# Six PSUM banks in one ring, token loads sent together, and new paces for the filler of a two-scan block

## The chip, the cores and the metric

One NeuronCore of one Trainium2 chip runs the kernel. The metric is the device time of one execution in microseconds. TensorE (PE), VectorE (DVE), ScalarE (ACT), GpSimd (POOL) and SyncE (SP, which here only issues DMA transfers) each take their own instructions in the order in which they stand in the program; they meet through semaphores.

## The reference

A layer of a backbone: 2048 tokens and a prefix of 256 context tokens, 1024 channels. After an adaptive norm one projection `w_in` gives the inputs of three mixers and of a gate; the mixers' outputs, times the gate, go through `w_out`.

```
p = (layer_norm(x) * (1 + scale) + shift) @ w_in      # also for ctx
pv, u, fh, g = split(p)
y = rwkv7_scan(shift3(u), 2 directions)               # state (64 x 64) per head, 6 heads
    S = S*w - (S kk) (kk*a)^T + v k^T ;  y = S r
o = hgrn2_scan(fh, 2 directions)                      # chunks of a gated linear attention, 6 heads
    S = exp(g_last)*S + (k exp(g_last - g))^T i
mix = concat(pool(pv), readout(y), rms(o)) * silu(g)
out = layer_norm(ALPHA*x + gate * (mix @ w_out))
```

## The kernel before

Products in float32 are made of three products of split operands (high by high, low by high, high by low): a block of 128 channels by up to 512 tokens is 24 matmuls over eight k tiles. There are four stages. The first (to 511 us) projects what the first scan needs and computes its chunk factors. The second (511 to 1395) is the rwkv scan: 2304 tokens in 36 chunks of 64, both directions in the same step. The third (to 1926) is the hgrn scan in ten windows, n = 0 to 9. The fourth reads out, norms, gates and multiplies by `w_out`.

**The filler.** The rest of the projection, 22 blocks of weights by three parts of 768 tokens, runs on PE beside both scans (`filler`, matmuls at L567, PSUM tile `fps` in a ring of two of its own). It hands over six matmuls at a time. At the beginning of a part it splits the part's tokens: for each of the eight k tiles a load into `fxs` (two buffers, L529), a ScalarE cast into `fxh` (L213) and a DVE subtraction into `fxl` (L214). The load for k + 2 is issued once k is split; the last two load the next part's first ones. Weights come as `fwf` (512 KB, one buffer, L217), cast by ScalarE, subtracted by POOL into `fwl`. Sinks of two kinds transpose on PE (L597 and L626) through a bank of the scan.

**The scan.** An iteration n runs step n, and prepares later chunks: `start` makes the scores of a chunk seven steps ahead (matmuls at L720, two banks `pa` a direction, each emptied by a masked copy of DVE at L722 into `at`); `gather` writes blocks of them out and `solve` inverts them for four chunks together on DVE (L777 multiplies, L780 adds, some 62 instructions a group), spread over two iterations in portions of seven between PE's work; `merge` (L829, L839) completes the inverse on PE for the next step; `late` transposes keys (L742). Seven iterations, n = -7 to -1, stand before step 0. `step` begins with the `py` matmuls (L856, L862), then `pu` (L872), the state `zp` (L881) and the output `y2` (L897). PSUM has eight banks: `psa` (scores, merge, transposes), `psy`, `psu` and the filler's ring have two each. An allocation in a ring waits until the tile that many allocations before it is read.

**Order.** PE's order is written by hand (`manual_schedule`): the loop over n calls the generators in turn, and `pace` runs the filler by a share of `R_FIL[1]` at four points of an iteration (0.22, 0.34, 0.22, 0.22), so many portions of six matmuls. `R_FIL[0]` portions run before the loop. The other engines' orders are set by a scheduler.

**The hgrn scan.** A window has fourteen slots; each slot runs parts of `hlevels` (scores `pl`, L1043) and `hsteps` (transposes `kt`, outputs `po` at L1102 and L1105, state products `ps` at L1115, added to `sbd` by DVE at L1120), then the filler by `H_FIL`. `po` is filled over two steps, copied by ScalarE into `os` (L1109) and sent by POOL's queue (L1110). In window 8 the rest of the filler runs at slot 0, then `out_weights`: for each of eight blocks a load of `w_out` into `fwf` (L1131), times the gate on POOL (L1132), a split by ScalarE and DVE into the tiles of the filler's tokens (768 columns) and into own ones (256). The readout loads with `ya`, `yb`, `oa`, `ob` (L1214), the gate `gt` (L1227) and the pooled part `mx` (L1233), which DVE multiplies (L1234).

## Time and profile before

| | us |
|---|---|
| median of three runs | 2161.99 (2156.2 to 2167.65) |
| profiled execution | 2169.2 |
| its span, first to last instruction | 2167.3 |
| PE busy | 1866.9 (86%) |
| DVE busy | 1439.7 (66%) |
| ScalarE busy | 930.9 (43%) |
| POOL busy | 797.8 (37%) |

The profiled execution is 0.33% above the median. Its span leaves out 1.9 us around the first and the last instruction. The mean granted clock of PE is 0.909 of full speed. Busy shares are means over stages with different limits: the questions are, for each stage, which engine is busiest and what PE waited for last. A wait is written under the instruction that waited, with the one that released it; the idle time in brackets in a timeline is that of the engine before the row.

### The profile page before, as it was taken

What the parts mean: (1) busy time and instruction counts of PE and PEld (TensorE: products, weight loads), DVE (VectorE), ACT (ScalarE), POOL (GpSimd) and SP (SyncE); (2) the same over time, 40 slices, a digit from 0 to 9 for tenths busy, and PEclk for the clock granted to TensorE, in tenths of its full rate; (3) what the DMA queues carried; (4) which work ended last, traced back from release to release, by engine and by line L of the source; (5) the groups of instructions that cost most, each with busy time, mean ns of one, the idle gap of its engine ahead of it and who ended that gap; (6) DMA issues with size and microseconds to landing.
All of it is one profiled execution on the core that took longest, in us unless ns stands there. A gap on an engine that the chain in (4) does not pass through costs nothing.

```text
span 2167.3 us, 46917 instructions
## 1 busy us (share of the span) xinstructions
PE 1866.9 (86%) x18498; PEld 1581.6 (73%) x18498; DVE 1439.7 (66%) x3037; ACT 930.9 (43%) x1763; POOL 797.8 (37%) x729
## 2 busy tenths in 40 slices
PE   3788899994979988989889897989999998869996
PEld 1677788892857767878768775877787877758886
DVE  2678898885266475675484763167976777669762
ACT  3876786653213333333323233445455555223331
POOL 0144355545211332232232331454443445324653
PEclk7899999996989998999989897999998995589998
DMA  6544444327545567556545544443232333346531
GB/s 245 183 143 146 141 129 126 106 74 237 163 132 149 165 173 202 154 167 177 151 133 167 141 117 139 142 131 90 78 105 80 98 108 109 124 141 199 184 127 59
DMA packets 285156, 305.32 MB, mean 141 GB/s; under 512 B 84932, under 2 KB 243780, under 8 KB 283912
## 3 DMA queue, kind: packets, MB, share of 16 engines
q1 hardware_dynamic: 274920, 271.90, 42.1%
q10 hardware_dynamic: 4896, 17.83, 2.4%
q0 software_dynamic: 5120, 12.59, 1.9%
q8 instruction: 146, 2.39, 0.5%
q14 instruction: 74, 0.61, 0.1%
HBM read 205.49 MB, written 96.74 MB: 139 GB/s over the span
## 4 chain that ended last, share of the span: by engine, by line
PE 33%; DVE 23%; DMA 9%; issue 4%; ACT 3%; POOL 3%; SPq 1%; POOLq 0%; DVEq 0%; ACTq 0%
PE fps L567 14%; DVE o L780 5%; DVE tm L777 4%; PE po L1278 2%; PE pl L1043 2%; DVE sbd L1120 2%; PE po L1105 1%; DMA m<-sd 1%; DVE tot L1075 1%; PE po L1102 1%; DVE at L722 1%; PE py L856 1%; DMA nn<-so 1%; PE pa L720 1%; DVE ml L1222 1%
## 5 line engine op out<-in xcount | busy, mean ns | idle before, releaser
L214 POOL TENSOR_TENSOR fwl<-fwf,fwh 128x1024 fp32r<-128x1024 f32 x66 | 160.1, 2426 | 398.1 <-ACT fwh L213 299.0
L567 PE MATMUL fps<-fxh,fwh 128*128 128x256 f32 (+1 forms) x952 | 228.6, 374 | 29.8 <-ACT fxh L213 22.1
L567 PE MATMUL fps<-fxl,fwh 128*128 128x256 f32 (+1 forms) x952 | 222.1, 365 | 0.0
L567 PE MATMUL fps<-fxh,fwl 128*128 128x256 f32 (+1 forms) x952 | 214.5, 360 | 0.4 <-POOL fwl L214 0.4
L567 PEld LDWEIGHTS fps<-fxh,fwh 128*128 128x128 f32 x952 | 159.1, 200 | 60.5 <-ACT fxh L213 25.5
L567 PEld LDWEIGHTS fps<-fxl,fwh 128*128 128x128 f32 x952 | 160.8, 199 | 27.2 <-issue 4.6
L567 PEld LDWEIGHTS fps<-fxh,fwl 128*128 128x128 f32 x952 | 159.4, 198 | 25.9 <-issue 0.7
L1120 DVE SCALAR_TENSOR_TENSOR sbd<-sbd,tot,ps 64x64 f32<-64x64 f32 x432 | 120.4, 279 | 54.4 <-PE ps L1115 44.1
L1038 ACT COPY qb<-qp 64x384 f32<-64x384 f32 x192 | 99.8, 520 | 120.9 <-PE pl L1043 90.2
L902 POOL TENSOR_TENSOR ys<-ys,pp 64x384 f32<-64x384 f32 x64 | 74.1, 1158 | 199.5 <-ACT ys L899 187.7
L330 PE MATMUL ps<-xh,wh 128*128 128x258 f32 x768 | 125.6, 304 | 18.1 <-ACT wh L213 12.4
L780 DVE TENSOR_TENSOR o<-o,tm 96x31 f32<-96x31 f32 (+15 forms) x279 | 130.6, 468 | 8.1
L777 DVE TENSOR_TENSOR tm<-m,o 96x31 f32<-96x31 f32 (+15 forms) x279 | 109.6, 393 | 36.6 <-DMA m<-sd 29.0
L330 PEld LDWEIGHTS ps<-xh,wh 128*128 128x128 f32 x768 | 106.1, 198 | 31.3 <-ACT wh L213 13.8
L722 DVE TENSOR_TENSOR at<-pa,cst 128x384 f32<-128x384 f32 x144 | 74.1, 548 | 78.3 <-PE pa L720 78.0
L330 PE MATMUL ps<-xh,wl 128*128 128x258 f32 x768 | 118.9, 294 | 0.0
L1072 POOL TENSOR_TENSOR ks<-ks,tot 128x384 f32<-128x384 f32 x90 | 86.3, 964 | 86.5 <-PE pl L1043 78.9
L330 PE MATMUL ps<-xl,wh 128*128 128x258 f32 x768 | 116.2, 290 | 0.0
L1043 PE MATMUL pl<-qb,ks 128*64 128x64 f32 x2304 | 102.4, 248 | 13.4 <-POOL ks L1072 9.9
L821 DVE STREAM_TRANSPOSE nn<-nn 32x192 f32<-32x192 f32 x36 | 13.2, 367 | 146.6 <-DMA nn<-so 138.1
L330 PEld LDWEIGHTS ps<-xh,wl 128*128 128x128 f32 x768 | 104.9, 196 | 5.7 <-issue 5.2
L1043 PEld LDWEIGHTS pl<-qb,ks 128*64 128x64 f32 x2304 | 88.6, 158 | 24.7 <-POOL ks L1072 10.5
(230 smaller groups left out, 4441.9 us busy)
## 6 DMA issues: line engine op xcount, KB each, us to landing
fwf<-in_w_in_dram SPq DMA_DIRECT2D x66, 512.0 KB, 4.1
xt<-in_x_dram ACTq DMA_DIRECT2D x32, 512.0 KB, 5.0
s_kr<-kr SPq DMA_DIRECT2D x54, 256.0 KB, 2.4
s_bk<-bk SPq DMA_DIRECT2D x54, 256.0 KB, 2.5
bks<-s_bk SPq DMA_DIRECT2D x72, 192.0 KB, 2.8
krs<-s_kr SPq DMA_DIRECT2D x72, 192.0 KB, 3.0
bk<-s_bk SPq DMA_DIRECT2D x72, 192.0 KB, 2.7
kr<-s_kr SPq DMA_DIRECT2D x72, 192.0 KB, 3.2
```

The costliest lines, as they stand in the source:

```text
L214: eng.tensor_tensor(out=wl, in0=wf, in1=wh.bitcast(F32), op=ALU.subtract)
L330: PE.matmul(ps[:, 0:TG + 2], a[:, k, :], b[:, k, :], start=(i == 0), stop=(i == 23))
L567: PE.matmul(ps[:, 0:n], a[:, k, :], b[k][:, o:o + n], start=(i == 0), stop=(i == 23))
L722: V.tensor_tensor(out=at[:, h], in0=pa[h], in1=cst[:, C_MASK[d]].unsqueeze(1).broadcast_to([P, NPR, P]), op=ALU.mult)
L777: V.tensor_tensor(out=tv, in0=m[:, j:j + 1, j + 1:32].broadcast_to([nrow, na, nb]), in1=o[:, 0:na, j:j + 1].broadcast_to([nrow, na, nb]), ...
L780: V.tensor_tensor(out=o[:, 0:na, j + 1:32], in0=o[:, 0:na, j + 1:32], in1=tv, op=ALU.subtract)
L902: G.tensor_tensor(out=ys[vr], in0=ys[vr], in1=pp[d][vr], op=ALU.add)
L1038: S.copy(out=qb[hh, :, :, h, :].rearrange("q p c (i b) -> q (p c) i b", b=b), in_=src[hh].rearrange("q p (c i j b) -> q (p c) i j b", c=nc ...
L1043: PE.matmul(pl[64 * (c % 2):64 * (c % 2) + 64, :, p, c // 2, :], ks[:, p, CH * c:CH * c + CH], qb[:, p, c, :, :], start=True, stop=True)
L1072: eng.tensor_tensor(out=v_, in0=v_, in1=tv[:, :, :, 1 - par:2 - par].broadcast_to([P, NPR, nb, b]), op=ALU.mult)
L1120: V.scalar_tensor_tensor(out=sn[hh, p, hh], in0=so_[hh, p, hh], scalar=tot[hh, p, c:c + 1], in1=ps[hh, p, :], op0=ALU.mult, op1=ALU.add)
L1278: PE.matmul(po, mix[k][a][:, tj], wo[k, 0][b][:, 0:512], start=(i == 0), stop=(i == 23))
```

## The change

Four things change.

One: in the rwkv scan `psa`, `psy` and `psu` become one ring of six banks, from which scores, merges, transposes, `py`, `pu`, `zp` and `y2` are taken in the order of the program. In the hgrn scan `psl`, `psk`, `pso` and `pss` become one ring of six. The filler's own two banks stay.

Two: in the filler the first two k tiles of a part are loaded into `fxs` as before; the six others are loaded into the tiles `fxl` themselves, all at once, and split in place; the next part's first two are loaded after the second split.

Three: the paces. `R_FIL` is 10 before step 0 and 7.1 from it, for 7.6; `H_FIL` is 2.0, 1.8 and 0.85 for 2.2, 1.9 and 1.0. In PE's order this makes 540 filler matmuls before step 0 for 438 (221,184 columns for 175,104), of them 312 before the scores of the fourth chunk for 264 (129,024 columns for 110,592) and 198 from there to the first merge for 150 (76,800 for 56,832). Between the first and the last step they are 1440 for 1548 (580,608 columns for 628,224). In a window of the hgrn scan from the fourth on they are 72 for 84, and the last one stands at the beginning of window 8 for that of window 7. The first L720 stands behind 120 of them in both.

Four: `out_weights` is two generators. Columns 768 to 1024, into own tiles, run in windows 4 and 5, the others behind the filler's end, with loads of 384 KB for 512. The gate row has a tile of its own and is loaded at the stage's beginning. `os` has one buffer for two.

```
-R_FIL = (20, 7.6)
-H_FIL = (2.2, 1.9, 1.0)
+R_FIL = (20, 10, 7.1)
+H_FIL = (2.0, 1.8, 0.85)
...
-        xs = [load(parts[0], k) for k in range(2)]
+        def ahead(part):
+            return [load(part, k, fp.tile([P, FTOK], F32, name="fxs", bufs=2)) for k in range(2)]
+        xs = ahead(parts[0])
...
+            xh = [big.tile([P, FTOK], F32R, name=f"fxh{k}") for k in range(KB)]
+            xl = [big.tile([P, FTOK], F32R, name=f"fxl{k}") for k in range(KB)]
+            src = xs + [load(part, k, xl[k].bitcast(F32)) for k in range(2, KB)]
             for k in range(KB):
-                xh.append(big.tile([P, FTOK], F32R, name=f"fxh{k}"))
-                xl.append(big.tile([P, FTOK], F32R, name=f"fxl{k}"))
-                split(xs[k % 2][:, 0:n_all], xh[k][:, 0:n_all], xl[k][:, 0:n_all], V)
-                if k + 2 < KB:
-                    xs[k % 2] = load(part, k + 2)
-                elif pi + 1 < len(parts):
-                    xs[k % 2] = load(parts[pi + 1], k % 2)
+                split(src[k][:, 0:n_all], xh[k][:, 0:n_all], xl[k][:, 0:n_all], V)
+                if k == 1 and pi + 1 < len(parts):
+                    xs = ahead(parts[pi + 1])
...
-        psa = ph.enter_context(tc.tile_pool(name="psa", bufs=2, space=PSUM, reuse_waits="tile"))
-        psy = ph.enter_context(tc.tile_pool(name="psy", bufs=2, space=PSUM, reuse_waits="tile"))
-        psu = ph.enter_context(tc.tile_pool(name="psu", bufs=2, space=PSUM, reuse_waits="tile"))
+        psa = ph.enter_context(tc.tile_pool(name="psa", bufs=6, space=PSUM, reuse_waits="tile"))
+        def bank(shape, **k):
+            return psa.tile([P, 512], F32, name="pa")[:, 0:NPR * P].rearrange(shape, **k)
...
-                py.append(psy.tile([P, NPR, 2, CH], F32, name="py"))
+                py.append(bank("q (p h e) -> q p h e", p=NPR, h=2))
...
-            pace(k * R_FIL[1])
+            pace(k * R_FIL[1 if n < 0 else 2])
...
-        psl = ph.enter_context(tc.tile_pool(name="psl", bufs=2, space=PSUM, reuse_waits="tile"))
-        pst = ph.enter_context(tc.tile_pool(name="psk", bufs=1, space=PSUM, reuse_waits="tile"))
+        pst = ph.enter_context(tc.tile_pool(name="psk", bufs=6, space=PSUM, reuse_waits="tile"))
-        pso = ph.enter_context(tc.tile_pool(name="pso", bufs=1, space=PSUM, reuse_waits="tile"))
-        pss = ph.enter_context(tc.tile_pool(name="pss", bufs=2, space=PSUM, reuse_waits="tile"))
...
-                        os_ = stp.tile([P, 384], F32, name="os")
+                        os_ = stp.tile([P, 384], F32, name="os", bufs=1)
...
-        def out_weights():
-            gtb = fp.tile([P, KB, P], F32R, name="fwh", bufs=2).bitcast(F32).rearrange("q k c -> q (k c)")
-            SP.dma_start(out=gtb, in_=s_gate.partition_broadcast(P))
+        gtb = bigl.tile([P, D], F32, name="gtb")
+        SP.dma_start(out=gtb, in_=s_gate.partition_broadcast(P))
+        def out_weights(j):
+            pool, nm_, c = ((big, "fx", slice(0, FTOK)), (bigl, "wo", slice(FTOK, D)))[j]
+            n = c.stop - c.start
             for k in range(KB):
...
+                wf = fp.tile([P, KB, P], F32, name="fwf").rearrange("q k c -> q (k c)")[:, 0:n]
+                SP.dma_start(out=wf, in_=w_out[P * k:P * k + P, c])
+                G.tensor_tensor(out=wf, in0=wf, in1=gtb[:, c], op=ALU.mult)
...
+                    if n in (4, 5) and si % 3 == 1:
+                        run(ow1, 1)
...
+            run(ow1)
             run(ow)
```

How this stands in the engines' rows is shown at three places. First SP where the filler begins, at about 502 us of the trace. `fwf<-in_w_in_dram` is the filler's first load of weights, `fxs` and `fxl` are loads of tokens, `bks` and `krs` are operands of the first scores, `s_kr`, `s_bk` and `s_bon` are written by the first stage. Before:

```order
L217 DMA fwf<-in_w_in_dram 128x1024
L432 DMA s_bon<-t 128x256
L415 DMA s_kr<-kr 128x4x128
L529 DMA fxs<-s_x 128x256
L529 DMA fxs<-s_x 128x512
L416 DMA s_bk<-bk 128x4x128
L415 DMA s_kr<-kr 128x4x128
L529 DMA fxs<-s_x 128x256
L529 DMA fxs<-s_x 128x512
L416 DMA s_bk<-bk 128x4x128 x2
L432 DMA s_bon<-t 128x256
L529 DMA fxs<-s_x 128x256
```

After:

```order
L528 DMA fxl_6036<-s_x 128x512
L528 DMA fxl_6037<-s_x 128x256
L528 DMA fxl_6037<-s_x 128x512
L528 DMA fxs<-s_x 128x256
L528 DMA fxs<-s_x 128x512
L528 DMA fxs<-s_x 128x256
L528 DMA fxs<-s_x 128x512
L711 DMA bks_6005<-s_bk 128x384
L712 DMA krs_6004<-s_kr 128x384
L711 DMA bks_6010<-s_bk 128x384
L712 DMA krs_6009<-s_kr 128x384
L217 DMA fwf<-in_w_in_dram 128x1024
```

The first load of weights stood ahead of the loads of six token tiles; it now stands behind all of them, behind the next part's first two k tiles and behind four loads of the scan.

Second SP at the border ahead of the filler's last part. `bk`, `kr` and `uv` are loads of the scan, `so` is written by a solve and `s_g` by the filler. Before:

```order
L529 DMA fxs<-s_x 128x512
L529 DMA fxs<-s_x 128x256
L529 DMA fxs<-s_x 128x512
L586 DMA s_g<-fe 128x512
L529 DMA fxs<-s_x 128x256
L733 DMA bk_15339<-s_bk 128x384
L733 DMA bk_15343<-s_bk 128x384
L783 DMA so<-o 96x1024
L529 DMA fxs<-s_x 128x512
L529 DMA fxs<-s_x 128x256
L734 DMA kr_15555<-s_kr 128x384
L217 DMA fwf<-in_w_in_dram 128x1024
```

After:

```order
L588 DMA s_g<-fe 128x512
L528 DMA fxl_15225<-s_x 128x512
L528 DMA fxl_15225<-s_x 128x256
L528 DMA fxl_15226<-s_x 128x512
L528 DMA fxl_15226<-s_x 128x256
L528 DMA fxl_15227<-s_x 128x512
L528 DMA fxl_15227<-s_x 128x256
L528 DMA fxl_15228<-s_x 128x512
L528 DMA fxl_15228<-s_x 128x256
L737 DMA bk_15319<-s_bk 128x384
L737 DMA bk_15323<-s_bk 128x384
L814 DMA uv_15389<-s_vt 64x384
```

The token loads stood one by one among the scan's transfers, each behind the split that freed its buffer; now the twelve loads of six k tiles stand in a row (four of them ahead of the piece shown), and the loads of the scan behind them.

Third DVE at the end of the hgrn scan. `fxl<-fwf,fxh` is the last split of the output weights, `sbd` the state updates, `mx<-mx,gt` the product of pooled part and gate for the readout. Before, where window 8 is still running:

```order
L1045 COPY_PREDICATED sc_21085<-cst,pl 128x384
L1072 TENSOR_TENSOR qp_21080<-qp_21080,tot_21352 128x96x4
L1120 SCALAR_TENSOR_TENSOR sbd_16282<-sbd_16281,tot_21104,ps 64x64 x6
L1234 TENSOR_TENSOR mx<-mx,gt 128x512 x2
L1045 COPY_PREDICATED sc_21079<-cst,pl 128x192x2
L1072 TENSOR_TENSOR qp_21074<-qp_21074,tot_21406 128x48x8
L1120 SCALAR_TENSOR_TENSOR sbd_16281<-sbd_16282,tot_21104,ps 64x64 x6
```

After, at the last updates of window 9:

```order
L214 TENSOR_TENSOR fxl_21515<-fwf,fxh_21514 128x768
L1124 SCALAR_TENSOR_TENSOR sbd_16241<-sbd_16240,tot_21669,pa 64x64 x6
L1124 SCALAR_TENSOR_TENSOR sbd_16240<-sbd_16241,tot_21669,pa 64x64 x6
L1124 SCALAR_TENSOR_TENSOR sbd_16243<-sbd_16242,tot_21689,pa 64x64 x6
L1124 SCALAR_TENSOR_TENSOR sbd_16242<-sbd_16243,tot_21689,pa 64x64 x6
L1124 SCALAR_TENSOR_TENSOR sbd_16241<-sbd_16240,tot_21669,pa 64x64 x6
L1242 TENSOR_TENSOR mx<-mx,gt 128x512
L1124 SCALAR_TENSOR_TENSOR sbd_16240<-sbd_16241,tot_21669,pa 64x64 x6
L1242 TENSOR_TENSOR mx<-mx,gt 128x512
L1124 SCALAR_TENSOR_TENSOR sbd_16243<-sbd_16242,tot_21689,pa 64x64 x6
L1124 SCALAR_TENSOR_TENSOR sbd_16242<-sbd_16243,tot_21689,pa 64x64 x6
```

The two products of `mx` stood ahead of most of window 8's work; they now stand between the last updates of the state, behind the last split of the output weights.

## Rows read from the trace of the kernel before

**Rows 1.** Busy us (instructions) of each engine in three stretches, PE clock, DMA share.

```profile
core 0: us, PE busy (x) PEld busy (x) DVE busy (x) ACT busy (x) POOL busy (x), PEclk, DMA share, GB/s
...
511.00:559.00 48.00, 31.04 (x124) 23.84 (x126) 7.55 (x20) 10.29 (x14) 13.09 (x14) 0.73 0.62 194
...
652.00:1395.00 743.00, 651.46 (x7949) 545.61 (x7948) 443.37 (x993) 246.70 (x521) 206.64 (x183) 0.94 0.55 155
1395.00:1926.00 531.00, 484.52 (x5707) 401.84 (x5706) 374.88 (x867) 250.53 (x445) 229.96 (x194) 0.87 0.32 100
```

**Rows 2.** Waits of PE in the scan: us in total, times, longest.

```profile
PE pa L829 <- DVE at L722: 31.4, 12, 5.4
PE pa L829 <- DVE nn L821: 11.7, 1, 11.7
PE pa L720 <- DVE at L722: 10.0, 11, 2.4
PE pa L626 <- DVE at L722: 9.4, 3, 4.3
PE pa L597 <- DVE at L722: 7.8, 3, 4.2
```

**Rows 3.** Timeline of PE: start, us, instruction; in brackets idle time before it.

```profile
652.07 1.50 PE L856 MATMUL py<-zbd,kr 128*128 128x128 f32 x12
...
965.94 0.57 PE L829 MATMUL pa<-nn,at 32*32 32x32 f32 x24 [3.44 <-DVE at L722]
...
1388.67 1.50 PE L856 MATMUL py<-zbd,kr 128*128 128x128 f32 x12
```

**Rows 4.** Timeline of DVE inside one step with an inversion.

```profile
956.60 0.55 DVE L722 TENSOR_TENSOR at<-pa,cst 128x384 f32<-128x384 f32 x1
957.07 1.04 DVE L780 TENSOR_TENSOR o<-o,tm 96x231 f32<-96x231 f32 x1
958.03 0.54 DVE L722 TENSOR_TENSOR at<-pa,cst 128x384 f32<-128x384 f32 x1
...
965.35 1.01 DVE L722 TENSOR_TENSOR at<-pa,cst 128x384 f32<-128x384 f32 x2
```

**Rows 5.** Groups of the page: the inversion of the solves.

```profile
L780 DVE TENSOR_TENSOR o<-o,tm 96x31 f32<-96x31 f32 (+15 forms) x279 | 130.6, 468 | 8.1
L777 DVE TENSOR_TENSOR tm<-m,o 96x31 f32<-96x31 f32 (+15 forms) x279 | 109.6, 393 | 36.6 <-DMA m<-sd 29.0
```

**Rows 6.** Timeline of PE at the beginning of the filler.

```profile
544.29 1.98 PE L567 MATMUL fps<-fxh,fwh 128*128 128x512 f32 x8
546.11 1.98 PE L567 MATMUL fps<-fxh,fwl 128*128 128x512 f32 x8
...
558.84 0.94 PE L720 MATMUL pa<-krs,bks 64*128 64x128 f32 x12
```

**Rows 7.** Timeline of PE at the borders between the filler's parts.

```profile
802.18 1.64 PE L567 MATMUL fps<-fxl,fwh 128*128 128x512 f32 x6
...
828.33 2.08 PE L567 MATMUL fps<-fxh,fwh 128*128 128x256 f32 x8
...
1293.76 1.98 PE L567 MATMUL fps<-fxl,fwh 128*128 128x512 f32 x8
...
1328.64 3.62 PE L567 MATMUL fps<-fxh,fwl 128*128 128x512 f32 x8
```

**Rows 8.** The same columns as the first group, in window 7.

```profile
1780.00:1840.00 60.00, 53.61 (x562) 44.71 (x560) 43.05 (x98) 28.37 (x53) 28.55 (x21) 0.52 0.36 108
```

**Rows 9.** Timeline of POOL: first and last multiplication of the output weights.

```profile
1744.86 2.37 POOL L1132 TENSOR_TENSOR fwf<-fwf,fwh 128x1024 f32<-128x1024 f32 x1 [5.24 <-DMA s_g<-fe]
...
1836.60 2.35 POOL L1132 TENSOR_TENSOR fwf<-fwf,fwh 128x1024 f32<-128x1024 f32 x1 [2.67 <-DVE tot L1075]
```

**Rows 10.** The tile os: duration in ns; its transfers to landing.

```profile
L1109 ACT COPY os<-po x32: 462/479/481, 1523.4 to 1924.9; 128x384 f32<-128x384 f32 x32
...
DMA to landing us min/median/max: 2.1/3.2/5.4
```

More of the change, by code (lines that the diff above doesn't have):

```diff
@@ L523, in filler, with load @@
     def filler(parts, blocks):
-        def load(part, k):
-            xs = fp.tile([P, FTOK], F32, name="fxs", bufs=2)
+        def load(part, k, xs):
             o = 0
@@ L867, in step @@
             yield 1
-            pu = psu.tile([P, NPR, 2, CH], F32, name="pu")
+            pu = bank("q (p h e) -> q p h e", p=NPR, h=2)
             for p, h in heads_:
@@ L877, in step @@
             if n + 1 < NCH:
-                zp = psu.tile([P, 2, NPR, CH], F32, name="pu")
+                zp = bank("q (d p e) -> q d p e", d=2, p=NPR)
                 for d in range(2):
@@ L891, in step @@
             if lat:
-                y2 = psu.tile([P, NPR, 2, CH], F32, name="pu")
+                y2 = bank("q (p h e) -> q p h e", p=NPR, h=2)
                 for p, h in heads_:
@@ L1039, in scores @@
                            in_=src[hh].rearrange("q p (c i j b) -> q (p c) i j b", c=nch, j=2, b=b)[:, :, :, par, :])
-                pl = psl.tile([P, 2, NPR, nm, CH // 2], F32, name="pl")
+                pl = bank(384, "q (h p m t) -> q h p m t", h=2, p=NPR, m=nm)
                 for p in range(NPR):
@@ L1050, in hlevels @@
             if lat:
-                pd = [psl.tile([P, NPR, nm, CH], F32, name="pl") for _ in range(2)]
+                pd = [bank(384, "q (p m t) -> q p m t", p=NPR, m=nm) for _ in range(2)]
                 for h in range(2):
@@ L1098, in hsteps @@
                     if s % 2 == 0:
-                        po = pso.tile([P, NPR, 2, CH], F32, name="po")
+                        po = bank(384, "q (p h e) -> q p h e", p=NPR, h=2)
                     for p in range(NPR):
@@ L1107, in hsteps @@
                     if s % 2 == 1:
-                        os_ = stp.tile([P, 384], F32, name="os")
+                        os_ = stp.tile([P, 384], F32, name="os", bufs=1)
                         S.copy(out=os_, in_=po.rearrange("q p h e -> q (p h e)"))
                         QO.dma_start(out=s_o[d, t0 + P * m:t0 + P * m + P, :], in_=os_)
-                ps = pss.tile([P, NPR, CH], F32, name="ps")
+                ps = bank(192, "q (p e) -> q p e", p=NPR)
                 for p in range(NPR):
```

18 lines of the change are left out of this document (7 added, 11 removed).

## The prediction, made before the changed kernel was run

> **What bounds the kernel now.** I read the table of stages first: in which stage is the matmul engine (PE) idle, and which other engine is as long? Over the scan of 36 steps, 652 to 1395 us, PE is busy 651.46 of 743 us, VectorE (DVE) 443.37, the others far less [rows 1]. So PE is the longest engine and stands idle for 91.5 us; in the second scan (1395 to 1926) it is idle for 46.5. In the stretch in which the filler begins, 511 to 559, it is idle for 17 us. Next the waits of PE: which ended last? In the scan the largest is L829, the first matmul of a merge, for the L722 copies of DVE: 31.4 us in 12 waits. The filler's own transposes at L626 and L597 wait for the same copies, 9.4 and 7.8, and the score matmuls at L720 10.0: together 58.6 us [rows 2]. L829 does not read what L722 writes; it asks for a PSUM bank that L722 has to empty, and the ring "psa" has two banks, so that each request waits for the one but one ahead of it. Then the timelines: L829 at 965.94 stood 3.44 us [rows 3], while DVE issued the copies of one chunk at 956.60, 958.03 and 965.35, each between pieces of the inversion (tm, o) [rows 4]. So PE waits for a copy that lies on a busy DVE behind work that nobody waits for at that moment.
>
> The length of a step: the first step begins at 652.07 and the last at 1388.67 [rows 3], 736.6/35 = 21.05 us. DVE's floor in a step with an inversion: L777 and L780 take 130.6 + 109.6 = 240.2 us [rows 5] for nine groups, 26.7 a group, spread over two steps, 13.3 each. What else DVE does in the scan is 443.4 less eight groups, 230 us or 6.4 a step. So 19.7 us for a step that inverts (16 of them), and no step of that kind can be much under 20. The others are bounded by PE.
>
> **The change part by part.** The price of a filler product of 512 columns: eight start at 544.29 and the next eight at 546.11 [rows 6], 1.82/8 = 0.2275 us.
>
> *Start, to the first score matmuls at 558.84* [rows 6]: 0. Products stand there for tokens now, and the tokens' loads go out at once after the change; but by the order they, the next part's four loads and four of the scan stand ahead of the first weight load on SP, which stood far ahead before. Earlier tokens meet later weights, and the same 120 matmuls lie ahead of the first L720. The 17 idle us bound it [rows 1]; half of them either way, -8 to +8, is an estimate.
>
> *Products before step 0*: 438 become 540, by columns +46,080, or 46,080/512 x 0.2275 = 20.5 us. The solve of the first group begins with the fourth chunk; 18,432 more columns lie ahead of that, +8.2, and nothing hides them. From there to the first merge 19,968 more lie beside the solve, whose end PE awaited for 11.7 us [rows 2]: 8.9 us of products fit into that and cost nothing. Of the last 7,680 (3.4 us) I take 1.5 as seen. Lead-in +9.7; bounds +8 (all covered) and +20 (nothing covered).
>
> *The scan*: (a) 47,616 columns fewer between the first step and the last, 93 x 0.2275 = -21. (b) The ring of six banks: thirteen requests an iteration, so that a request waits for the sixth ahead of it. L829 and the filler's transposes then wait for the first direction's copies, not the second's, some 9 us sooner on DVE (956.60 against 965.35 [rows 4]). The 31.4, 9.4 and 7.8 are 48.6 us; the 10.0 of L720 stay, as its sixth is the copy just before. I take two thirds, -32: the rest comes back where DVE at its 19.7 us is behind anyway, as then the next request, the py of the next step, waits for the second direction's copies. (c) The borders between parts. Between the last product of part 0 at 802.18 and the first of part 1 at 828.33 lie 26 us, and between 1293.76 and 1328.64, where products run in a row again, 35 [rows 7]. Six of eight token loads now go out together instead of each after the split of the one two ahead of it. I take 20 us less in sum; but 12 issues in a row stand in SP's queue ahead of the scan's own loads (kr, uv, gathers), for which I give back 5: -15, bounds +5 and -30. (d) Clock: PE was granted 0.94 of full speed over the scan [rows 1], that is about 89 us of half clock, and half clock stands where PE had stood idle. With 50 us less idle: -5, bounds 0 and -20. Together -73. Bounds: -35 (waits move to the py, borders gain nothing) and -105 (nearly all idle time goes).
>
> *The second scan*: the paces fall, by 0.2 a slot in the first window, 0.1 in two and 0.15 from the fourth. By the order that last is 84 to 72 products a window; so some 80 products leave windows 0 to 6, and with the 12 that are left over from the first scan some 90 go into windows 7 and 8. -5 for the first three and -10 for the next four (48 products at 0.2 each). In window 7 before, 1780 to 1840, PE had no products and was granted 0.52 of its clock, [rows 8], against 0.87 over the whole of this stage [rows 1]. It took about 58 us at half clock; at full clock its own work is near 30 and 72 products add 16: -10. Window 8 gets some 20 products: +4. PE's waits for copies there fall with the shared ring: -6. (e) Three quarters of the output weights go through POOL, ScalarE and DVE only after the last product, so in window 8 and later: eight blocks, which before took from 1744.86 to 1836.60 [rows 9]; at 7.5 us each (less POOL work, 768 columns for 1024) 60 us from the beginning of window 8, ending some 10 us before the second scan's end instead of 80. The readout's tiles lie over theirs, and by the order DVE multiplies mx between the last updates of the state: +4, bounds 0 and +12. Together -23; bounds -8 and -45.
>
> **The sum**: 0 + 9.7 - 73 - 23 = -86.3, against the profiled execution: 2169.2 - 86.3 = 2082.9. The median of the runs, 2161.99, is 0.9967 of the profiled 2169.2, so 2076. Of the bounds, taken as independent, about 45 us remain to either side.
>
> **Rivals.** *DVE keeps PE waiting anyway.* The copies stay in DVE's row behind the inversion's pieces; if the second direction's copies are as late as before, py of the next step waits instead of L829. For it: in [rows 4] the copy of 956.60 is followed by an o of 1.04 us and the next copy starts only after it, in their order. Against it: py stands 6 to 7 us behind L829 with products between. Then the -32 and half of the borders' gain (7) are lost: -47, 2122 profiled, 2115. Beside this: the Trainium skill, "PSUM — Partial Sum Buffer", section "Engine vs sequencer instructions", says that the queues of ScalarE, VectorE and GpSimdE are strictly first in, first out. By that rule a larger ring cannot move a copy ahead of the inversion; the trace agrees (956.60, 957.07, 958.03 stand one behind the other), and it is why a third of (b) stays in my sum.
>
> *Work only moves.* PE is busy 88% in the scan, the number of products is the same, and what leaves the steps comes back in the lead-in: +20 there, -21 in the scan, the waits reappear under other names, and 10 us remain from the second scan. About 2158. Against it: the idle time is there to be filled.
>
> *Slower: the shared ring in the second scan.* A po bank is held over two steps and emptied by the ScalarE copy into os, which has one buffer now instead of two; so a copy must wait until the transfer of the copy before it has landed, 3.2 us in the median [rows 10], and the six-bank ring hands this to whatever PE asks for next. 32 copies x (3.2 + 0.5) = 118 us: 2082.9 + 118 = 2201, 2194 as a median. It decides from 86/32 = 2.7 us a copy. Against it: a copy would have to follow the one before within some 4 us to wait at all, and 32 copies between 1523.4 and 1924.9 [rows 10] lie 12.5 us apart in the mean.
>
> *Better*: nearly all of the scan's idle time goes and the clock holds: -140, 2022.
>
> **Chances.** Forecast 0.60, DVE 0.22, only moves 0.07, slower 0.05, better 0.06. The range from 2030 to 2130 takes in the forecast with its bounds and the DVE rival, and leaves out about 0.18. A measurement of this kernel can tell about 0.5% from no change: faster by more 0.88, within it 0.07, slower 0.05.
>
> **What would show it.** In the waits of PE: L829 behind L722 near nothing, py behind L722 under 20 us in sum. If py has 30 or more, the DVE rival holds. The first step near 662, and steps of 19 us in the mean up to the last. Borders of 15 to 20 us. PE at full clock through window 7. The first L720 within 8 us of 558.8. The last multiplication of the output weights some 10 us before the last po; if it is later and DVE's mx stands idle before the last sbd, (e) was too small. ScalarE's os copies waiting for their own transfers would speak for the slower rival. Wrong altogether it would be if the step stayed at 21 us with fewer products in it: then PE was not the bound.

## The result and the profile after

The changed kernel takes 2085.82 us in the median of four runs (2084.24 to 2086.05) against 2164.82 (2156.2 to 2168.75): a ratio of 0.9639, with an interval from 0.9607 to 0.9671. That is about 78 us less; the forecast was 2076. The profiled execution took 2086.04 us with a span of 2084.0. Where the time went, by the marks of the two traces:

| | before | after | difference | forecast |
|---|---|---|---|---|
| first score matmuls | 558.84 | 555.24 | -3.6 | 0 |
| step 0 | 652.07 | 658.95 | +6.9 | +9.7 |
| step 0 to step 35 | 736.6 | 672.9 | -63.7 | -73 |
| step 35 to the last state product | 536.2 | 504.0 | -32.2 | -27 |
| from there to the end | 242.4 | 248.2 | +5.8 | +4 |

The forecast's -23 for the second scan's stage is split here into its -27 and the +4 of the readout. Single profiles scatter in these rows. Five profiles of kernels with the changed code up to step 0 have the first scores at 554.3 to 557.3 and step 0 at 658.8 to 661.5; a second profile with the old code up to there has 556.4 and 650.6. So the -3.6 is about what single profiles differ by, and the +6.9 may be 9. The busy us of each engine (PE, weight loads, DVE, ScalarE, POOL, each with its instructions), the granted clock of PE, the DMA share and GB/s in three stretches of the changed kernel, to be held against [rows 1]:

```profile
511.00:555.00 44.00, 28.02 (x120) 21.68 (x120) 4.40 (x15) 9.31 (x12) 11.91 (x5) 0.83 0.58 187
...
659.00:1332.00 673.00, 613.70 (x7743) 518.45 (x7742) 439.49 (x988) 235.29 (x504) 199.74 (x182) 0.94 0.59 167
1332.00:1836.00 504.00, 477.04 (x5798) 395.02 (x5797) 370.18 (x864) 250.21 (x445) 231.78 (x200) 0.90 0.35 107
```

In the first scan PE is idle for 59 us instead of 91, and busy for 38 us less in these stretches (32 from step 0 to step 35); in the second its idle time fell from 46 to 27. What PE waited for in the first scan (us in total, times, longest), which answers to [rows 2]:

```profile
PE pa L724 <- DVE at L726: 17.5, 5, 5.1
PE pa L628 <- DVE fe L625: 13.5, 2, 7.4
PE pa L876 <- ACT pp L870: 11.9, 9, 3.9
PE pa L833 <- DVE nn L825: 9.8, 2, 6.2
```

L833 (L829 before) no longer waits for the copies (L726, before L722) at all. The scores at L724 wait for them longer than before, 17.5 against 10.0. The timeline of PE shows the beginning, the first merge, the two borders, and the first and last step, as [rows 3, 6, 7] do for before:

```profile
522.12 3.68 PE L569 MATMUL fps<-fxh,fwh 128*128 128x512 f32 x8 [13.85 <-ACT fwh L213]
...
525.64 2.02 PE L569 MATMUL fps<-fxh,fwl 128*128 128x512 f32 x8
...
555.24 0.94 PE L724 MATMUL pa<-krs,bks 64*128 64x128 f32 x12
...
646.75 0.28 PE L833 MATMUL pa<-nn,at 32*32 32x32 f32 x2 [6.17 <-DVE nn L825]
...
658.95 1.50 PE L860 MATMUL pa<-zbd,kr 128*128 128x128 f32 x12
...
757.57 1.66 PE L569 MATMUL fps<-fxl,fwh 128*128 128x512 f32 x6
...
776.28 2.04 PE L569 MATMUL fps<-fxh,fwh 128*128 128x256 f32 x8
...
1248.41 2.00 PE L569 MATMUL fps<-fxl,fwh 128*128 128x512 f32 x8
...
1271.86 2.65 PE L569 MATMUL fps<-fxh,fwh 128*128 128x512 f32 x8
...
1331.82 1.39 PE L860 MATMUL pa<-zbd,kr 128*128 128x128 f32 x11
```

PE stands 13.85 us for the first block of weights, which the tokens now precede, and the first scores come 3.6 us earlier all the same. The wait for the first solve is 6.17 instead of 11.7. From the start of the last product of a part to the start of the first of the next it is 17.5 and 21.8 us, against 24.9 and 23.7 before (the second was followed by single products until 1328.64).

### The profile page after: what moved, and what is told of

It reads as the page before. It is cut to its first block, busy times and chain, and to the rows that moved or that the text cites. A ratio compares the mean times of both kernels' runs of the same rounds, so it can differ in the third digit from the quotient of the medians.

```text
span 2084.0 us, 47024 instructions
## 1 busy us (share of the span) xinstructions
PE 1841.7 (88%) x18498; PEld 1563.7 (75%) x18498; DVE 1433.6 (69%) x3037; ACT 927.0 (44%) x1762; POOL 799.7 (38%) x737
## 4 chain that ended last, share of the span: by engine, by line
PE 40%; DVE 17%; DMA 7%; issue 5%; POOL 3%; ACT 3%; SPq 1%; POOLq 0%; ACTq 0%; DVEq 0%
PE fps L569 17%; DVE tm L781 2%; DVE o L784 2%; PE po L1286 2%; PE pa L1047 2%; PE pa L724 2%; PE pa L860 2%; DVE sbd L1124 2%; PE pa L876 1%; PE pa L1109 1%; PE pa L866 1%; PE pa L1106 1%; DVE tot L1079 1%; DMA fwf<-in_w_out_dram 1%; DMA fwf<-in_w_in_dram 1%
## 5 line engine op out<-in xcount | busy, mean ns | idle before, releaser
L569 PEld LDWEIGHTS fps<-fxh,fwh 128*128 128x128 f32 x952 | 157.1, 198 | 54.5 <-ACT fwh L213 18.8
L781 DVE TENSOR_TENSOR tm<-m,o 96x31 f32<-96x31 f32 (+15 forms) x279 | 123.3, 442 | 38.3 <-DMA m<-sd 30.5
L1124 DVE SCALAR_TENSOR_TENSOR sbd<-sbd,tot,pa 64x64 f32<-64x64 f32 x432 | 120.5, 279 | 38.4 <-PE pa L1119 28.3
L726 DVE TENSOR_TENSOR at<-pa,cst 128x384 f32<-128x384 f32 x144 | 74.2, 548 | 75.1 <-PE pa L724 74.7
L784 DVE TENSOR_TENSOR o<-o,tm 96x31 f32<-96x31 f32 (+15 forms) x279 | 114.6, 411 | 8.0
L1076 POOL TENSOR_TENSOR ks<-ks,tot 128x384 f32<-128x384 f32 x90 | 86.6, 967 | 76.5 <-PE pa L1047 66.4
L330 PEld LDWEIGHTS ps<-xl,wh 128*128 128x128 f32 x768 | 102.8, 193 | 4.9 <-issue 4.6
L1047 PE MATMUL pa<-qb,ks 128*64 128x64 f32 x2304 | 94.5, 236 | 9.0 <-POOL ks L1076 6.4
L404 POOL TENSOR_TENSOR kr<-t 128x256 f32<-128x256 f32 x54 | 47.4, 878 | 134.0 <-ACT t L391 74.9
```

What stands on the lines that cost most here:

```text
L330: PE.matmul(ps[:, 0:TG + 2], a[:, k, :], b[:, k, :], start=(i == 0), stop=(i == 23))
L404: G.tensor_tensor(out=kr[:, :, pr], in0=c4(kk), in1=e_k, op=ALU.mult)
L569: PE.matmul(ps[:, 0:n], a[:, k, :], b[k][:, o:o + n], start=(i == 0), stop=(i == 23))
L726: V.tensor_tensor(out=at[:, h], in0=pa[h], in1=cst[:, C_MASK[d]].unsqueeze(1).broadcast_to([P, NPR, P]), op=ALU.mult)
L781: V.tensor_tensor(out=tv, in0=m[:, j:j + 1, j + 1:32].broadcast_to([nrow, na, nb]), in1=o[:, 0:na, j:j + 1].broadcast_to([nrow, na, nb]), ...
L784: V.tensor_tensor(out=o[:, 0:na, j + 1:32], in0=o[:, 0:na, j + 1:32], in1=tv, op=ALU.subtract)
```

## The experiments

Twelve kernels, one of them the changed kernel once more, were run in three groups, each beside the kernel before on the same chip. The first group takes one part out of the changed kernel, the second puts one part alone into the kernel before, the third asks about the end, the start and the second scan's paces. Their stages, in us of one profiled execution each:

| kernel | step 0 at | first scan | second scan | behind it | ratio to before (interval) |
|---|---|---|---|---|---|
| before | 652.1 | 736.6 | 536.2 | 242.4 | 1 |
| changed | 659.0 | 672.9 | 504.0 | 248.2 | 0.9639 (0.9607 to 0.9671) |
| changed, old rings | 661.2 | 690.1 | 505.5 | 244.1 | 0.9721 (0.9669 to 0.9773) |
| changed, old pace of the scan | 649.1 | 694.1 | 518.5 | 241.2 | 0.9694 (0.9646 to 0.9741) |
| changed, old token loads | 661.2 | 678.7 | 507.9 | 243.3 | 0.9658 (0.9607 to 0.9708) |
| changed, old second scan | 661.5 | 673.1 | 540.7 | 241.0 | 0.9733 (0.9679 to 0.9788) |
| before, new ring alone | 649.1 | 705.2 | 540.3 | 239.7 | 0.9884 (0.9856 to 0.9912) |
| before, new pace alone | 663.1 | 696.8 | 520.5 | 240.6 | 0.9824 (0.9785 to 0.9862) |
| before, new loads alone | 649.1 | 721.9 | 530.0 | 239.2 | 0.9920 (0.9892 to 0.9948) |
| before, new second scan alone | 650.6 | 731.1 | 519.3 | 244.0 | 0.9900 (0.9873 to 0.9926) |
| changed, again | 661.2 | 674.2 | 502.5 | 241.4 | 0.9626 (0.9595 to 0.9658) |
| changed, os in the fwh tiles | 661.5 | 673.2 | 502.2 | 263.1 | 0.9720 (0.9691 to 0.9749) |
| the same, first weights ahead | 657.6 | 670.1 | 501.6 | 259.4 | 0.9686 (0.9652 to 0.9720) |
| changed, old paces of the second scan | 658.8 | 670.8 | 493.0 | 240.5 | 0.9590 (0.9552 to 0.9629) |

One unit of 0.001 is 2.2 us. The second scan's stage is from step 35 to the last state product. How far a single profile can be trusted, the rows with equal code show: the old first scan took 736.6 and, with only the second scan changed, 731.1 us; the changed one 670.8 to 674.2 in five profiles with the same code up to there; the old second scan 520.5 to 540.7 in five.

### One part taken out

**The scan's rings.**

```
-        psa = ph.enter_context(tc.tile_pool(name="psa", bufs=6, space=PSUM, reuse_waits="tile"))
+        psa = ph.enter_context(tc.tile_pool(name="psa", bufs=2, space=PSUM, reuse_waits="tile"))
+        psy = ph.enter_context(tc.tile_pool(name="psy", bufs=2, space=PSUM, reuse_waits="tile"))
+        psu = ph.enter_context(tc.tile_pool(name="psu", bufs=2, space=PSUM, reuse_waits="tile"))
...
-                py.append(bank("q (p h e) -> q p h e", p=NPR, h=2))
+                py.append(psy.tile([P, NPR, 2, CH], F32, name="py"))
```

> The changed kernel with the scan's three old PSUM rings of two banks (psa, psy, psu) in place of the ring of six; all else stays changed. My theory (the ring takes two thirds of 48.6 us of waits): 2086 + 32 = about 2118, L833 waits again behind the copies at L726 for 25 to 35 us in sum. Rival, DVE keeps PE waiting anyway: within 8 us of 2086, the L833 waits come back but the waits at L724 and L860 go. Rival, the ring is worth more than its waits because the idle time also costs clock: above 2130.

It took 2103.48 us, and the first scan 690.1 against 672.9: 17 us, half of what I expected and more than the rival that DVE holds PE anyway allowed. The waits of PE in the scan of this kernel:

```profile
PE pa L835 <- DVE at L728: 32.1, 12, 4.7
...
PE pa L726 <- DVE at L728: 7.3, 9, 1.9
PE pa L599 <- DVE at L728: 6.8, 2, 5.1
PE pa L628 <- DVE fe L625: 3.5, 2, 2.5
```

The waits of the merge (L835 here) come back to 32.1 us, as large as before the change, and those of L599 with them. So the mechanism is the one that I named, and 39 us of waits return; but the stage gets only 17 longer, since the waits at the scores fall from 17.5 to 7.3 and those at L628 for `fe` from 13.5 to 3.5. Of the 17 us, 10.5 are idle time of PE and 6.7 busy time for the same products.

**The scan's pace.**

```
-R_FIL = (20, 10, 7.1)
+R_FIL = (20, 7.6, 7.6)
```

> The changed kernel with the scan's old pace, 7.6 of portions in each iteration before and after step 0; the second scan's paces stay changed. By columns 46,080 move from before step 0 into the 35 steps. My theory: step 0 about 7 us earlier (659 to 652), the steps 21 us longer in sum, so 2086 + 14 = 2100. Rival, the solve chain or DVE and not PE sets the steps that invert: less than 6 us slower, since the products go into waits. Rival, work only moves: 2086.

2098.24 us. Step 0 came 9.9 us earlier and the 35 steps took 21.2 us longer, which is the price of the columns moved, 0.2275 us for 512 of them. That the products go into waits, and that work only moves, fall. The second scan, whose code is the changed one, took 518.5 us in this profile for 504.0; it is the longest of the kernel's four runs (2105.04).

**The token loads.**

```
-            src = xs + [load(part, k, xl[k].bitcast(F32)) for k in range(2, KB)]
             for k in range(KB):
-                split(src[k][:, 0:n_all], xh[k][:, 0:n_all], xl[k][:, 0:n_all], V)
-                if k == 1 and pi + 1 < len(parts):
-                    xs = ahead(parts[pi + 1])
+                split(xs[k % 2][:, 0:n_all], xh[k][:, 0:n_all], xl[k][:, 0:n_all], V)
+                if k + 2 < KB:
+                    xs[k % 2] = load(part, k + 2, fp.tile([P, FTOK], F32, name="fxs", bufs=2))
...
```

> The changed kernel with the tokens loaded one k tile after the other through two buffers as before. My theory: the borders get 15 us longer in sum (from 17.5 and 21.8 us back to 25 and 24 to 35), the first score matmuls stay within 5 us of 555: 2086 + 15 = 2101. Rival, the issues in a row cost as much as the early tokens bring: 2086 within 4 us.

2089.88 us, 4 us more by the ratios, which lies inside the intervals. The first scan is 5.8 us longer; the gaps at the borders are 18.4 and 24.2 us. The term of 15 us is not there when the other parts are.

**The second scan.** The stage's whole code is that of before (four rings, paces 2.2, 1.9 and 1.0, one generator for the output weights, two `os` buffers).

```
+        psl = ph.enter_context(tc.tile_pool(name="psl", bufs=2, space=PSUM, reuse_waits="tile"))
+        pst = ph.enter_context(tc.tile_pool(name="psk", bufs=1, space=PSUM, reuse_waits="tile"))
+        pso = ph.enter_context(tc.tile_pool(name="pso", bufs=1, space=PSUM, reuse_waits="tile"))
+        pss = ph.enter_context(tc.tile_pool(name="pss", bufs=2, space=PSUM, reuse_waits="tile"))
...
```

> The changed kernel with the whole second scan stage of before: its four PSUM rings, its paces, the output weights in one generator, two os buffers. My theory: what I put on this stage, 23 us, comes back, and the 5.8 us that the stretch behind it got longer go: 2086 + 26 = 2112, from the last step of the first scan to the last state product 536 us as before against 504. Rival, most of the stage's gain is a clock that hangs on how the first scan ends and not on this stage's code: under 2095.

2105.78 us, 20 more by the ratios; in the profiled execution, which is the longest of its four runs (2118.16), the stage took 540.7. So most of the stage's gain is its own code's. That the first scan has a part in it too shows with the pace alone, below.

### One part alone

The four taken out cost 18, 12, 4 and 20 us, 54 in sum, where all together bring 78. So I put each alone into the kernel before. The edits are the reverse of those above.

**The ring.**

```
-        psa = ph.enter_context(tc.tile_pool(name="psa", bufs=2, space=PSUM, reuse_waits="tile"))
+        psa = ph.enter_context(tc.tile_pool(name="psa", bufs=6, space=PSUM, reuse_waits="tile"))
...
```

> The kernel before with the ring of six banks in the scan alone. Undoing the four parts one by one cost 18, 12, 4 and 20 us, 54 in sum, where the whole change brought about 80. Theory, the parts share the same idle time (what one leaves, another takes): alone each brings more than its undoing cost, the ring about 32 as predicted: 2165 - 32 = 2133. Rival, the parts need each other: alone the ring brings 18 or less, 2147 or more.

2136.59 us, 25 less by the ratio, and the first scan is 31.4 us shorter, the size of my term of 32. But that term was idle time, and PE's idle time fell by 22.5 us only (90.9 to 68.4); the other 8.9 are busy time for the same products, with 75.1 us at half clock for 95.6. The merge no longer waits for the copies, while PE's wait for the first solve grew to 16.9 us, the waits at the scores to 27.3 and those of `pu` for ScalarE's copy `pp` from 2.0 to 11.9.

**The pace.**

```
-R_FIL = (20, 7.6)
+R_FIL = (20, 10, 7.1)
...
-            pace(k * R_FIL[1])
+            pace(k * R_FIL[1 if n < 0 else 2])
```

> The kernel before with the new pace of the first scan alone (10 before step 0, 7.1 after). Theory, shared idle time: step 0 8 us later, the steps 21 us and more shorter: 15 to 25 us faster, about 2145. Rival, they need each other: with the old rings the iterations wait for DVE however few products they hold: at most 12 us faster, 2153 or more.

2122.85 us, 38 less: twice what the theory said. The first scan is 39.8 us shorter, 28.5 of that in PE's busy time, of which the columns explain 21, and 11.3 in its idle time, with 31.1 us of merge waits still there. Some of it lies in single steps: the third went from 29.8 to 20.4 us, the eighth from 30.5 to 18.3, and the one with the second border from 35.0 to 26.6, while the first grew from 16.5 to 27.9 and the sixth from 22.7 to 28.1. Much of this is moved between neighbours: the first three together went from 69.3 to 66.4. The second scan, whose code was not touched, is 15.7 us shorter too, at a granted clock of 0.91 against 0.87. Why other points for the same products shorten these steps by so much was not settled.

**The token loads.**

```
-            xs[k % 2] = load(part, k + 2)
+            src = xs + [load(part, k, xl[k].bitcast(F32)) for k in range(2, KB)]
...
```

> The kernel before with the token loads sent together, alone. Before, the gaps at the borders were 25 and 24 to 33 us. Theory, shared idle time: both fall to some 18 to 20 us and 10 to 15 us are gained, about 2152. Rival, they need each other: 4 us or less, as in undoing it, 2161 or more.

2145.48 us, 17 less. The first scan is 14.7 us shorter (11.2 of it idle time), the size of the term that I had put on it; most is in the step with the second border, 26.3 against 35.0. But the gaps without any product, which I expected at 18 to 20, are nearly as long as before, 23.4 and 23.1 us. With the ring alone they are 18.7 and 22.5: what shortens the first gap is the ring.

**The second scan.**

```
-        pso = ph.enter_context(tc.tile_pool(name="pso", bufs=1, space=PSUM, reuse_waits="tile"))
+        pst = ph.enter_context(tc.tile_pool(name="psk", bufs=6, space=PSUM, reuse_waits="tile"))
...
```

> The kernel before with the second scan's stage of the change alone (ring of six, paces, split output weights, one os buffer). The stages follow one another, so I expect what undoing it cost, 20 us: 2145, with 504 to 510 us from the last step to the last state product. Rival, its gain hangs on the first part of the change: less than 12 us.

2140.49 us, 22 less, like the 20 of its undoing. The stage took 519.3 us, where I expected 504 to 510; the profile is of the longest of the four runs (2147.21).

The four alone bring 25, 38, 17 and 22 us, 102 in sum, against 78 together and 54 by undoing. In the first scan alone it is 31.4, 39.8 and 14.7, 86 us, against 63.7 together and 44 by undoing. The pairs tell which parts share their gain, as each kernel with one part taken out holds the other two. Ring and loads (the changed kernel with the old pace) bring 42.5 us of the 46.1 that they bring alone: they add up nearly. Ring and pace bring 57.9 of 71.2, loads and pace 46.5 of 54.5. So it is the pace that the others share with. Alone it brings 39.8, and beside the other two 21.2, the price of its columns.

### The end, the start, and the paces of the second scan

**The changed kernel again**, to compare the next three with on the same chip.

> The changed kernel itself, on the chip and beside the runs of the two that follow, to compare them with: 2086 within 5 us, and 248 us from the last state product to the end.

2081.46 us. Behind the last state product it took 241.4 us, 6.8 less than in the first profile of the same kernel.

**The os copies of window 9.** In the changed kernel the tile `os` shows this (what its instructions waited for, us and times):

```profile
  DMA s_o<-os: 4.2, 1
```

```
-                        os_ = stp.tile([P, 384], F32, name="os", bufs=1)
+                        os_ = (stp.tile([P, 384], F32, name="os", bufs=1) if n < T // HWIN else
+                               fp.tile([P, KB, P], F32R, name="fwh", bufs=2)
+                               .bitcast(F32).rearrange("q k c -> q (k c)")[:, 0:384])
```

> The changed kernel, but the four os copies of window 9 go into the two fwh tiles, which are free by then, so that no copy waits for the transfer of the one before. In the changed kernel two of these four copies stand on ScalarE behind a cast of the readout (mh), the last waited 4.16 us for a transfer, and the readout's sq stood behind it. Theory: this is the 5.8 us that the end got longer: 4 to 6 us faster than the changed kernel, 2081. Rival, the readout waits for the late loads of ya, yb, oa, ob and not for ScalarE: within 1.5 us of it.

2101.64 us, 20 us slower. The edit made a wait of its own: the readout's tiles lie over the tiles `fwh`, so that their loads could not be issued before the copies had left. PE's first product of the readout in this kernel, and SP's first load for it:

```profile
1863.47 0.80 PE L1287 MATMUL po<-fxh,mh 128*128 128x512 f32 x1 [26.23 <-ACT mh L1230]
```

```profile
1842.98 0.37 SPq L1223 DMA_DIRECT2D ya<-s_y  x1
```

In the changed kernel SP issued the load of `ya` at 1805.21 and those of `yb`, `oa` and `ob` at 1811.67 to 1812.78, ahead of the last state product. So the run doesn't tell what the wait of 4.2 us costs. The repetition of the changed kernel says more: there the last copy waited 4.0 us for a transfer too, and another 6.7, and it has 241.4 us behind the last state product. So the 5.8 us of the first profile are no cost of that wait.

**The first weights ahead of the tokens.**

```
         xs = ahead(parts[0])
+        first = fp.tile([P, KB, P], F32, name="fwf")
+        QW.dma_start(out=first, in_=w_in[blocks[0][0]])
```

> The same as the run of the os copies, and the filler's first block of weights is loaded ahead of the token loads of k = 2 to 7. In the changed kernel PE stood 13.85 us for the cast of that block, until 522.12. Theory: the first score matmuls come 5 to 8 us before 555 and the rest follows: 5 to 8 us faster than the run of the os copies, 2075. Rival, the weights take the tokens' share of the transfers and the tokens come later by as much: within 2 us.

2092.05 us, 9.6 less than the run of the os copies, with ratios of 0.9686 and 0.9720 whose intervals meet. The first scores came 3.3 us earlier (553.98), step 0 3.9 and the last state product 7.7 (1829.27 against 1836.93); but the kernel with the old paces of the second scan (below), in which these loads stand as in the changed kernel, has its first scores at 554.3 and step 0 at 658.8, so that of the lead at step 0 little more than 1 us is sure. The timeline of PE:

```profile
512.15 2.69 PE L573 MATMUL fps<-fxh,fwh 128*128 128x512 f32 x5
...
517.90 0.80 PE L573 MATMUL fps<-fxh,fwh 128*128 128x512 f32 x1 [3.06 <-ACT fxh L213]
...
536.73 2.69 PE L573 MATMUL fps<-fxh,fwh 128*128 128x512 f32 x8 [3.26 <-ACT fwh L213]
...
553.98 0.94 PE L728 MATMUL pa<-krs,bks 64*128 64x128 f32 x12
```

The first product stands at 512 now, 12 us earlier than in the run of the os copies (524.50) and 10 earlier than in the changed kernel. Then PE waits for single tokens, and 3.26 us for the third block of weights, and most of the head start is lost. A likely reason is the rival's, though its 2 us are passed: from 495 to 530 us the DMA engines are busy nearly all the time in this kernel (shares of 0.84 to 1.08), and until 522 in the changed one (0.94 to 1.06), so that what is sent earlier puts off something else.

**The paces of the second scan.**

```
-H_FIL = (2.0, 1.8, 0.85)
+H_FIL = (2.2, 1.9, 1.0)
```

> The changed kernel with the second scan's old paces (2.2, 1.9, 1.0), so that the filler ends a window earlier. Theory: window 7 goes without products again and PE's clock falls to half there: window 7 takes 10 to 14 us longer, windows 0 to 6 take 8 to 12 us longer, window 8 is 4 us shorter; in sum 10 to 15 us longer from the last step of the first scan to the last state product, 2086 + 10. Rival, the shared ring and not the pace gave this stage its gain: within 4 us of 2086.

2074.56 us, 7 us faster than the changed kernel on the same chip (0.9590 against 0.9626, with intervals that overlap), where I expected 10 slower. It is the fastest kernel of the study; together with the first weights ahead it was not run. The stage took 493.0 us against 504.0 and 502.5. The last windows, first of the changed kernel (window 7, then 8 and 9 together), then of this one, with the columns of [rows 1]:

```profile
1714.60:1758.00 43.40, 43.04 (x649) 35.78 (x648) 37.41 (x94) 26.05 (x46) 16.57 (x17) 1.00 0.22 68
1758.00:1835.80 77.80, 71.91 (x714) 59.77 (x714) 45.68 (x116) 17.15 (x31) 33.72 (x27) 0.54 0.41 134
```

```profile
1707.90:1761.10 53.20, 42.14 (x589) 33.96 (x588) 45.58 (x104) 28.34 (x51) 28.95 (x24) 0.76 0.36 114
1761.10:1822.70 61.60, 55.61 (x715) 45.73 (x714) 37.85 (x110) 11.39 (x24) 21.08 (x20) 0.74 0.33 115
```

The new paces do hold the clock in window 7, 43.4 against 53.2 us, which is the gain of 10 that I forecast. They pay more than that behind it: windows 8 and 9 take 77.8 us at 0.54 of the clock against 61.6 at 0.74. And windows 0 to 6, where fewer products should have saved 15, took 382.8 us against 378.3. The late products and the output weights behind them push the stretch in which PE has little to do to the end, and it is then slower as a whole.

So with the old paces the stage has 493 us in the new code and 541 in the old. The 48 us are the most that can be had: the profile of the new code is the shortest of its four runs (2065.22) and that of the old the longest; by the ratios it is 31. Windows 4, 6, 7 and the last two hold 14.6, 6.4, 7.3 and 14.4 of the 48, and 38 are busy time for the same products, that is clock. Window 4 shows how that comes about, and how little it can be relied on. The kernel before (the waiting instruction, then three stretches of 10 us):

```profile
1641.85 0.91 PE L1102 MATMUL po<-it,sc 64*64 64x64 f32 x12 [2.69 <-ACT os L1109]
```

```profile
1640.00:1650.00 10.00, 8.15 (x76) 7.17 (x77) 7.41 (x20) 6.12 (x12) 2.52 (x3) 0.65 0.06 22
1650.00:1660.00 10.00, 10.00 (x101) 8.52 (x100) 4.49 (x14) 4.29 (x7) 3.84 (x3) 0.50 0.09 33
1660.00:1670.00 10.00, 10.00 (x103) 7.74 (x105) 5.94 (x16) 2.44 (x5) 4.13 (x4) 0.82 0.39 113
```

The changed kernel with the old second scan, the same place:

```profile
1584.80 0.91 PE L1106 MATMUL po<-it,sc 64*64 64x64 f32 x12 [2.21 <-ACT os L1113]
```

```profile
1585.00:1595.00 10.00, 10.00 (x106) 8.74 (x106) 5.29 (x14) 3.63 (x8) 2.06 (x3) 0.57 0.13 48
1595.00:1605.00 10.00, 10.00 (x88) 8.75 (x86) 5.37 (x16) 2.92 (x6) 1.78 (x2) 0.50 0.06 22
1605.00:1615.00 10.00, 10.00 (x71) 7.87 (x70) 5.32 (x11) 2.05 (x4) 5.51 (x4) 0.50 0.38 125
```

And the changed kernel with the old paces alone:

```profile
1570.00:1580.00 10.00, 9.81 (x149) 8.24 (x147) 9.21 (x26) 8.63 (x16) 2.52 (x3) 1.00 0.29 100
1580.00:1590.00 10.00, 10.00 (x156) 8.59 (x152) 8.82 (x22) 5.19 (x10) 4.85 (x4) 1.00 0.18 55
1590.00:1600.00 10.00, 9.71 (x122) 7.26 (x120) 9.55 (x26) 2.65 (x6) 6.51 (x8) 1.00 0.26 81
```

The old ring of `po` has one bank, so that L1102 (L1106) must wait until ScalarE has copied the bank out into `os`: 2.69 and 2.21 us. In both traces PE's clock is at half right behind that wait, for 20 to 31 us with PE busy throughout, 10.00 of 10. With the shared ring of six the wait is not there, and in this profile the clock stays at 1.00. The window took 59.3 and 63.3 us in the old code and 48.7 in the new, at the same paces.

Two other traces say that the wait alone does not set the half clock. The kernel before with the pace of the first scan alone has the same code in this stage and the same wait, but only 3 us of half clock behind it:

```profile
1610.08 0.91 PE L1102 MATMUL po<-it,sc 64*64 64x64 f32 x12 [2.23 <-ACT os L1109]
```

```profile
1610.00:1620.00 10.00, 9.92 (x132) 8.77 (x132) 7.00 (x20) 4.92 (x11) 2.97 (x4) 0.83 0.19 68
1620.00:1630.00 10.00, 10.00 (x146) 8.28 (x145) 8.70 (x18) 3.95 (x7) 5.50 (x5) 1.00 0.26 76
```

All five profiles of the old code have this wait in window 4, at 2.21 to 2.70 us, with 3, 20, 20, 24 and 31 us of half clock behind it. And the changed kernel, with the ring of six, falls to half clock for 14 us in window 5, as it does in its repetition, behind three short waits for the state:

```profile
1616.40 0.43 PE L1109 MATMUL pa<-sbd,qp 128*64 128x128 f32 x2 [0.89 <-DVE sbd L1124]
1617.02 0.43 PE L1109 MATMUL pa<-sbd,qp 128*64 128x128 f32 x2 [0.19 <-DVE sbd L1124]
1617.64 0.55 PE L1109 MATMUL pa<-sbd,qp 128*64 128x128 f32 x2 [0.19 <-DVE sbd L1124]
```

```profile
1618.00:1628.00 10.00, 10.00 (x99) 8.64 (x99) 6.64 (x18) 9.90 (x17) 2.09 (x3) 0.50 0.11 38
```

With the new second scan alone it is 24 us at half clock behind waits of 0.31, 0.19 and 0.19. So the new ring takes the wait for `os` away, and with it one occasion for the clock to fall; it does not keep the clock up. What is the same in every profile is PE's idle time in this stage: 43 to 47 us in the five with the old code, 27 to 36 in the nine with the new.

## Why the prediction was right, and where it was not

**What bounds the kernel.** PE and its idle time, as I had read it. Of the rivals, "DVE keeps PE waiting anyway" fell in the form in which I gave it: py (L860) never waits for L726. But its reason is right. The Trainium skill's rule of strict queues ("PSUM — Partial Sum Buffer", section "Engine vs sequencer instructions") fits what is left: no ring moves a copy ahead of the inversion, and the waits at the scores behind the same copies rose from 10.0 to 17.5 us, and to 27.3 with the ring alone. My floor of 19.7 us for a step that inverts is a mean and no floor: in the changed kernel steps 6, 9, 13, 17, 25 and 29 (counted from 0), with 8 to 13 us of inversion each, took 16.2 to 17.8 us.

**Start and lead-in.** 0 and +9.7; measured -3.6, and +6.9 up to step 0. The counts of columns carried: 8.2 less 3.6 is 4.6, and the first merge came 4.4 us later (646.75 against 642.37). Within the scatter named above, 0 and +9.7 are met.

**The first scan, -73; measured -63.7.** My -73 was 47 us of idle time (the ring 32, the loads 15), 21 of columns and 5 of clock. From step 0 to step 35 PE's idle time fell by 31.6 us (90.9 to 59.3) and its busy time by 32.2. Of the busy time 21 are the columns, as by undoing; some 5 are the clock, at half for 85.3 us instead of 95.6; 6 I can't place. So columns and clock were right, and the step that failed is the idle time: 31.6 for 47. Each of the two terms looked right alone, -31.4 for -32 and -14.7 for -15, but that is luck, as idle time they are 22.5 and 11.2. Together, without the pace, they are 35.3, so they do not take from each other; each was too large. For the ring I had named 48.6 us of waits and given back a third, at py. The waits named do go, but more than a third comes back, and elsewhere: at the scores (10.0 to 27.3 with the ring alone), at the first solve (11.7 to 16.9) and at pu (2.0 to 11.9). The loads hardly shorten the gaps on which I had counted. These are single profiles, and the other one of the old first scan (731.1 us) has 83.8 us of idle time and not 90.9, so that each of these falls may be 7 us smaller.

**The second scan, -23 with the readout; measured -26.** The sum is right and its terms are not, so this agreement is luck. The first step that failed is the paces, for which I had -15 in the windows 0 to 6, -10 in window 7 and +4 in window 8. Against the kernel with the old paces it is +4.5, -9.8 and, with window 9, +16.2; in the medians the new paces cost 7 us, with intervals that overlap, but a gain of 21 lies outside them. The other step is the rest of the stage, the ring, the split of the output weights and one `os` buffer. I had -6 for it, the sum of PE's waits; it is 31 us by the ratios of the two kernels with the old paces (0.9733 and 0.9590, from two groups of runs). In the two profiles 10 us of the difference are idle time (42.9 against 33.2). The rest is clock, for which I had counted nothing outside window 7, and its cause stays open: over the stage the clock is 0.86 to 0.91 in the old code, 0.88 to 0.91 in the new with the new paces and 0.93 with the old ones, and the first scan's pace moves it too, with the stage 15.7 us shorter for the new pace alone and 14.5 longer for the old pace in the changed kernel. What belongs to the ring and what to the split weights was not tried apart.

**The readout, +4.** +5.8 in one profile, -1 in the other of the same kernel: no effect can be told. The last multiplication of the weights began at 1807.99, some 25 us ahead of the last output product, where I had 10, and mx did not hold up DVE. The slower rival is nearly absent: once, 4.2 us, a copy waited for the transfer of the one before, and in the repetition twice, 10.7 us in sum, far from 118.

## What to carry to other kernels

Before one adds up terms that all live on the same idle time, one asks which of them share it, and puts them in by pairs: here three parts that bring 86 us alone bring 64 together, two of them add up, and the third, the pace, shares with both. A wait that a change takes away is not yet time gained; one has to name what the engine waits for next. A stage's time at half clock is not to be put down to the one wait ahead of it before other profiles of the same code have been read. And work that is moved behind a stage's end to keep an engine busy has to be priced where it ends, not only where it begins.

## What the runs showed of the hardware

In the second scan one wait of PE of 2.2 to 2.7 us, in five profiles of the same code, is followed by 3 to 31 us at half clock, though PE is busy again at once. Three waits of 0.89, 0.19 and 0.19 us are followed by 14 us. A wait of 2.50 us in the kernel with the pace alone (L1102 at 1712.07) is followed by none. The wait of 13.85 us at the filler's beginning, in a stretch that had been at half clock since 495 us, is followed by half the pace for one group of eight products only (3.68 us, then 2.02). So how long a wait is does not say how long the half clock behind it lasts. The Trainium skill has a case of this kind ("TensorE: Matmul & The Clock Gate", section "A second HAM failure mode: psum-queue depth-cycling"): short idle times between groups of matmuls that cycle through PSUM banks make the clock swing. The traces here agree in kind: the clock falls behind short waits with the rings of before and with the ring of six. And the same code takes 2073.59 to 2085.04 us from run to run, 0.5%, with 241 or 248 us behind the last state product; a gain of a few us can't be told from a single profile.
